# The low half of every second weight chunk formed by an accumulating DMA, in the gate blocks of a hybrid encoder

## Chip, cores and metric

One core of a Trainium2 chip runs the kernel as one program. The metric is device time in microseconds (us), the median of runs on the chip. Engines are named as in the profile: PE is TensorE (PEld its weight loads), DVE VectorE, ACT ScalarE, POOL GpSimd, SP SyncE, which issues most DMAs.

## The reference

One layer of an encoder on 256 tokens of width 2048, all in float32: an RMS norm, a wide input projection, two token mixers (a chunkwise mLSTM in both directions and an RG-LRU in both directions), each projected back to the model width, merged by sigmoid gates of the normalised input, and an output projection with a final norm.

```python
h = _rms_norm(x, norm_g)
proj = jnp.einsum('bsd,dn->bsn', h, w_in)
q_p, k_p, v_p, o_p, za_p, gif_p, xb_p, zb_p, ga_p, gb_p = jnp.split(proj, cuts, axis=-1)
ya = _mlstm_branch(q_p, k_p, v_p, o_p, za_p, gif_p, b_if, head_g)
yb = _rglru_branch(xb_p, zb_p, conv_w, conv_b, w_rg, b_rg, lam)
ya = jnp.einsum('bsw,wd->bsd', ya, w_branch_a)
yb = jnp.einsum('bsw,wd->bsd', yb, w_branch_b)
merged = jax.nn.sigmoid(ga_p) * ya + jax.nn.sigmoid(gb_p) * yb
out = _rms_norm(x + jnp.einsum('bsd,de->bse', merged, w_out), final_g)
```

The change touches the weights of the last lines but one: the columns of `w_in` for the gates `ga` and `gb`, `w_branch_a` and `w_branch_b`.

## The kernel before

The weights are read once, 512 columns at a time (a block of 2048 x 512, 4 MB), each block as eight chunks of 128 partitions x 1024 float32 (two slices of 128 rows side by side, 512 KB). PE multiplies in a rounded float32 type, so every operand is split in two: a high half `hi`, the value converted to that type, and a low half `lo`, what the conversion left out. A product takes three matmuls: high by high, high by low, low by high.

`load_chunk` makes a chunk's halves: SP loads it into `raw` (five buffers, L107), ACT converts it into `whi` (L108), DVE subtracts, `wlo = raw - whi` (L109). `whi` and `wlo` have three buffers each. `block_nat` (L112 to L126) uses the chunks as moving operand: 12 matmuls of 512 columns a chunk (L123 to L125, two slices by two token tiles by three products), 96 a block, into two PSUM accumulators. `block_tr` does the same with the chunks as stationary operand. The pairs of `load_chunk` carry a priority in the order of the program (`urgent`), and the Tile framework's scheduler, from priorities and its own estimates, fixes the order on each engine, PE's included, and sets the semaphores. Each engine then runs its own list in order.

The stage concerned is the last but one. For j = 0 to 3 it runs the block GB(j) of `wi`, then `wb[j]`; then for j = 0 to 3 the block GA(j) of `wi`, then `wa[j]`: 16 calls of `block_nat`, 128 chunks. Before it stand the four ZB blocks of `block_tr`, after it three `block_nat` blocks of `wo` and the last columns. After a block ACT or DVE takes the two accumulators over (sigmoid, L631 and L645; products, L637, L650, L651), and small transposes of the merged result are put between the chunks (L660). The slot `PT` (128 x 4096 float32) holds the attention weights until the last mLSTM head and later the scale `fg` of the final norm (loaded at L672, scaled by POOL at L673, first read at L688).

Of the kernel before, what the change touches and what calls it, by code (L numbers as in the profile page):

```python
# [10 lines left out]
F32 = mybir.dt.float32  # L11
F32R = mybir.dt.float32r
AF = mybir.ActivationFunctionType
ALU = mybir.AluOpType
ACT = mybir.EngineType.Activation

P = 128
# [3 lines left out]
NB = 512  # L21
KC = 2
# [6 lines left out]
BLK_Q, BLK_K, BLK_V, BLK_O, BLK_Z, BLK_XB, BLK_ZB, BLK_GA, BLK_GB = 0, 2, 4, 8, 12, 16, 20, 24, 28  # L29


def f(ap):
    return ap.bitcast(F32)
# [3 lines left out]
def hybrid_encoder(ctx: ExitStack, tc: tile.TileContext, x, xt, pk, bif, fg, wg, wi, wr, wa, wb, wo, out):  # L37
    nc = tc.nc
    pe, act, dve, pool, sp = nc.tensor, nc.scalar, nc.vector, nc.gpsimd, nc.sync
# [3 lines left out]
    wp = ctx.enter_context(tc.tile_pool(name="wp", bufs=1))  # L43
# [6 lines left out]
    def name(n):  # L50
        uid[0] += 1
        return f"{n}_{uid[0]}"
# [4 lines left out]
    def sl(tag, dt=F32, cols=4096):  # L57
        return slot.tile([P, cols], dt, tag=tag, name=name("s" + tag))

    def aux():  # L60
        return paux.tile([P, NB], F32, tag="aux", name=name("aux"))

    def acc_pair():
        return [pacc.tile([P, NB], F32, tag="acc", name=name("acc")) for _ in range(2)]

    def urgent():
        uid[0] += 1
        return tc.high_priority(offset=HP - 30 * uid[0])
# [10 lines left out]
    last_dma, last_copy, last_sub = [None], [None], [None]  # L79

    def tick():
        for q in (queue, queue2):
            if q:
                c = q.pop(0)
                if c is not None:
                    c()
# [9 lines left out]
    def load_chunk(src, dst=None, tag="w", bufs=3, parts=1):  # L96
        with urgent():
            raw = wp.tile([P, KC * NB], F32, tag="raw", name=name("raw"), bufs=5)
            if dst is None:
                hi = wp.tile([P, KC * NB], F32R, tag=tag + "hi", name=name(tag + "hi"), bufs=bufs)  # L100
                lo = wp.tile([P, KC * NB], F32R, tag=tag + "lo", name=name(tag + "lo"), bufs=bufs)
            else:
                hi, lo = dst
            w = KC * NB // parts
            for i in range(parts):
                r = slice(i * w, (i + 1) * w)
                last_dma[0] = sp.dma_start(raw[:, r], src[:, r]).ins  # L107
                last_copy[0] = act.copy(hi[:, r], raw[:, r]).ins  # L108
                last_sub[0] = dve.tensor_sub(lo[:, r], raw[:, r], f(hi[:, r])).ins  # L109
        return hi, lo  # L110

    def block_nat(src, xhi, xlo):  # L112
        ps = acc_pair()
        for kq in range(KT // KC):
            tick()
            hi, lo = load_chunk(src[kq])
            for kk in range(KC):
                k = kq * KC + kk
                wh, wl = hi[:, kk * NB:(kk + 1) * NB], lo[:, kk * NB:(kk + 1) * NB]
                for tb in range(2):  # L120
                    o = k * S + tb * P
                    a, b = xhi(o, o + P), xlo(o, o + P)
                    pe.matmul(ps[tb], a, wh, start=(k == 0), stop=False)  # L123
                    pe.matmul(ps[tb], a, wl, start=False, stop=False)  # L124
                    pe.matmul(ps[tb], b, wh, start=False, stop=(k == KT - 1))  # L125
        return ps  # L126

    def block_tr(src, xhi, xlo, pre=()):
        ps = acc_pair()
        for kq in range(KT // KC):  # L130
            tick()
            hi, lo = pre[kq] if kq < len(pre) else load_chunk(src[kq])
            for kk in range(KC):
                k = kq * KC + kk
                a, b = xhi(k * S, (k + 1) * S), xlo(k * S, (k + 1) * S)
                for m in range(4):
                    o = kk * NB + m * P
                    wh, wl = hi[:, o:o + P], lo[:, o:o + P]
                    dst = ps[m // 2][:, (m % 2) * S:(m % 2 + 1) * S]
                    first = k == 0 and m % 2 == 0  # L140
                    last = k == KT - 1
                    pe.matmul(dst, wh, a, start=first, stop=False, skip_group_check=True)  # L142
                    pe.matmul(dst, wh, b, start=False, stop=False, skip_group_check=True)  # L143
                    pe.matmul(dst, wl, a, start=False, stop=last, skip_group_check=True)  # L144
        return ps

    def evac_split(dst_hi, dst_lo, ps):
        with urgent():
            act.copy(dst_hi, ps)
            dve.tensor_sub(dst_lo, ps, f(dst_hi))  # L150
# [14 lines left out]
    hhi, hlo = Cols([hhi_t], 4096), Cols([hlo_t], 4096)  # L165
# [371 lines left out]
    def head(h):  # L537
        vhi = hp.tile([P, 2 * NB], F32R, tag="vhi", name=name("vhi"))
        vlo = hp.tile([P, 2 * NB], F32R, tag="vlo", name=name("vlo"))
        ps = block_nat(wi[BLK_V + h], hhi, hlo)  # L540
        for tb in range(2):
            r = slice(tb * NB, (tb + 1) * NB)
# [4 lines left out]
        to = hp.tile([P, 2 * NB], F32, tag="to", name=name("to"))  # L547
        zz = hp.tile([P, 2 * NB], F32, tag="zz", name=name("zz"))
        ps = block_nat(wi[BLK_O + h], hhi, hlo)
        with urgent():  # L550
            for tb in range(2):
                act.activation(to[:, tb * NB:(tb + 1) * NB], ps[tb], AF.Sigmoid, scale=rstd[:, tb:tb + 1])
        ps = block_nat(wi[BLK_Z + h], hhi, hlo)
        with urgent():
            for tb in range(2):
# [50 lines left out]
    ybh, ybl = [], []  # L606
    for j in range(4):
        ps = block_tr(wi[BLK_ZB + j], hhi, hlo)
# [14 lines left out]
    ybh, ybl = Cols(ybh, 1024), Cols(ybl, 1024)  # L623
    yah, yal = Cols([yas["h"]], 4096), Cols([yas["l"]], 4096)

    sgb = sl("E")
    for j in range(4):
        ps = block_nat(wi[BLK_GB + j], hhi, hlo)
        with urgent():
            for tb in range(2):  # L630
                act.activation(sgb[:, (j * 2 + tb) * NB:(j * 2 + tb + 1) * NB], ps[tb], AF.Sigmoid,  # L631
                               scale=rstd[:, tb:tb + 1])
        ps = block_nat(wb[j], ybh, ybl)
        with urgent():
            for tb in range(2):
                v = sgb[:, (j * 2 + tb) * NB:(j * 2 + tb + 1) * NB]
                dve.tensor_mul(v, v, ps[tb])  # L637

    mht, mlt = [], []
    for j in range(4):  # L640
        tg = hp.tile([P, 2 * NB], F32, tag="to" if j % 2 == 0 else "zz", name=name("tg"))
        ps = block_nat(wi[BLK_GA + j], hhi, hlo)
        with urgent():
            for tb in range(2):
                act.activation(tg[:, tb * NB:(tb + 1) * NB], ps[tb], AF.Sigmoid, scale=rstd[:, tb:tb + 1])  # L645
        ps = block_nat(wa[j], yah, yal)
        with urgent():
            for tb in range(2):
                v = tg[:, tb * NB:(tb + 1) * NB]
                dve.tensor_mul(v, v, ps[tb])  # L650
            dve.tensor_add(tg, tg, sgb[:, j * 1024:(j + 1) * 1024])  # L651
        mht.append(sl(f"C{j}", F32R, 1024))
        mlt.append(sl(f"D{j}", F32R, 1024))

        def fin_m(half, j=j, tg=tg):
            pt = aux()
            for i in range(2):
                m = half * 2 + i
                for tb in range(2):
                    pe.transpose(pt[:, i * S + tb * P:i * S + (tb + 1) * P],  # L660
                                 tg[:, tb * NB + m * P:tb * NB + (m + 1) * P], ident)
            o = half * NB
            evac_split(mht[j][:, o:o + NB], mlt[j][:, o:o + NB], pt)

        queue.extend([None, None, lambda c=fin_m: c(0), lambda c=fin_m: c(1)])
# [24 lines left out]
    for j in range(3):  # L690
        ps = block_nat(wo[j], mh, ml)
# [5 lines left out]
    for kq in range(8):  # L697
        o = (kq % 4) * KC * NB
        ch.append(load_chunk(wo[3][kq], dst=[lw[(kq // 4) * 2 + i][:, o:o + KC * NB] for i in range(2)]))
    for tb, a, b, col in ((0, 0, NB, 3), (1, 0, S, 3), (1, S, NB, 4)):  # L700
        ps = aux()[:, :b - a]
        for k in range(KT):
            hi, lo = ch[k // KC]
            c = (k % KC) * NB
            wh, wl = hi[:, c + a:c + b], lo[:, c + a:c + b]
            o = k * S + tb * P
# [58 lines left out]
```

## Time and profile before

| | us |
|---|---|
| runs (2) | 1052.97 and 1053.48, median 1053.22 |
| profiled execution, span from first to last instruction | 1050.9 |
| PE busy | 1039.4 (99%) |
| DVE busy | 646.9 (62%) |
| ACT busy | 533.5 (51%) |
| POOL busy | 36.7 (3%) |
| DMA, mean | 190 GB/s |

The span does not hold what the device does before the first and after the last instruction; the runs' times do, hence the 2.3 us between them. The busy time of PE counts a matmul from its start to its modelled end, and matmuls overlap. A group of instructions is shown as line, engine, operation, output and inputs, shape and count, then its busy time and the mean of one in nanoseconds, then the idle time of the engine just before such instructions and what ended it ("<-"). In the timeline a row gives the start, the duration, the instruction and, in brackets, the idle time before it and its releaser.

### The profile page before, as it was taken

To read this page: it belongs to the slowest core of one execution; us is meant where nothing else is said; L and a number is where in the kernel's file an instruction comes from. 1 tells how busy PE (TensorE), PEld (TensorE's weight loads), DVE (VectorE), ACT (ScalarE), POOL (GpSimd) and SP (SyncE) were. 2 spreads that over 40 slices of the span, in tenths; PEclk is the share of its full clock that TensorE was granted. 3 is DMA by queue.
4 is the path that set the end of the run, shared out by engine and by line. 5 is a ranking of instruction groups with operands and counts; after the bars stand their busy time and mean duration, and the time that the engine had idled before them with its cause. 6 is when DMAs were issued, how large, how long until landed. Compare 5 with 4: busy or idle time off the path is not lost.

```text
span 1050.9 us, 14840 instructions
## 1 busy us (share of the span) xinstructions
PE 1039.4 (99%) x5876; PEld 914.9 (87%) x5876; DVE 646.9 (62%) x809; ACT 533.5 (51%) x689; POOL 36.7 (3%) x48
## 2 busy tenths in 40 slices
PE   9999999999999999999999999999999999999996
PEld 8999988898889888988999988888888888888886
DVE  6566785489549845974786654454454545545573
ACT  7535447765684658466644443434434344444461
POOL 2000000010001001000320000000000000000000
PEclk9999999999999999999999999999999999999999
DMA  9744545556655654664656556666666565667652
GB/s 339 254 158 143 180 159 185 163 182 198 196 161 167 198 197 160 187 214 161 200 181 184 180 194 195 191 197 191 191 199 192 190 186 188 192 194 261 198 201 80
DMA packets 55669, 199.39 MB, mean 190 GB/s; under 512 B 6192, under 2 KB 6448, under 8 KB 55216
## 3 DMA queue, kind: packets, MB, share of 16 engines
q1 hardware_dynamic: 55600, 198.44, 58.7%
q8 instruction: 46, 0.75, 0.3%
q14 instruction: 23, 0.19, 0.0%
HBM read 196.32 MB, written 2.10 MB: 189 GB/s over the span
## 4 chain that ended last, share of the span: by engine, by line
PE 97%; DVE 1%; issue 1%; DMA 0%; POOL 0%; POOLq 0%; ACT 0%; DVEq 0%; SPq 0%; ACTq 0%
PE acc L123 21%; PE acc L124 21%; PE acc L125 21%; PE acc L144 9%; PE acc L142 9%; PE acc L143 9%; PE aux L573 1%; PE aux L490 1%; PE aux L489 1%; PE aux L488 1%; PE aux L403 1%; DVE sC L522 1%; PE aux L708 0%; PE aux L709 0%; PE aux L285 0%
## 5 line engine op out<-in xcount | busy, mean ns | idle before, releaser
L109 DVE TENSOR_TENSOR wlo<-raw,whi 128x1024 fp32r<-128x1024 f32 (+1 forms) x345 | 420.6, 1220 | 354.3 <-ACT whi L108 353.8
L108 ACT CAST whi<-raw 128x1024 fp32r<-128x1024 f32 (+1 forms) x345 | 361.7, 1049 | 442.2 <-PE acc L125 302.7
L124 PE MATMUL acc<-wlo,sH 128*128 128x512 f32 x640 | 249.7, 390 | 0.0
L125 PE MATMUL acc<-whi,sL 128*128 128x512 f32 x640 | 249.4, 390 | 0.0
L123 PE MATMUL acc<-whi,sH 128*128 128x512 f32 x640 | 229.5, 390 | 0.0
L142 PE MATMUL acc<-sH,whi 128*128 128x256 f32 x768 | 218.4, 286 | 0.8 <-ACT whi L108 0.8
L143 PE MATMUL acc<-sL,whi 128*128 128x256 f32 x768 | 217.0, 284 | 0.0
L144 PE MATMUL acc<-sH,wlo 128*128 128x256 f32 x768 | 215.0, 285 | 1.3 <-DVE wlo L109 1.3
L142 PEld LDWEIGHTS acc<-sH,whi 128*128 128x128 f32 x768 | 148.0, 193 | 2.0 <-ACT whi L108 1.1
L143 PEld LDWEIGHTS acc<-sL,whi 128*128 128x128 f32 x768 | 148.0, 193 | 0.3
L144 PEld LDWEIGHTS acc<-sH,wlo 128*128 128x128 f32 x768 | 146.1, 192 | 2.2 <-DVE wlo L109 2.0
L125 PEld LDWEIGHTS acc<-whi,sL 128*128 128x128 f32 x640 | 120.2, 188 | 24.4
L124 PEld LDWEIGHTS acc<-wlo,sH 128*128 128x128 f32 x640 | 120.3, 188 | 23.7
L123 PEld LDWEIGHTS acc<-whi,sH 128*128 128x128 f32 x640 | 119.9, 188 | 24.1
L124 PE MATMUL acc<-wlo,sC 128*128 128x512 f32 x224 | 87.2, 389 | 0.0
L125 PE MATMUL acc<-whi,sD 128*128 128x512 f32 x224 | 87.2, 389 | 0.0
L123 PE MATMUL acc<-whi,sC 128*128 128x512 f32 x224 | 78.4, 389 | 0.0
L124 PE MATMUL acc<-wlo,sA 128*128 128x512 f32 x128 | 49.8, 389 | 0.0
L125 PE MATMUL acc<-whi,sB 128*128 128x512 f32 x128 | 49.8, 389 | 0.0
L125 PEld LDWEIGHTS acc<-whi,sD 128*128 128x128 f32 x224 | 42.1, 188 | 8.7
L124 PEld LDWEIGHTS acc<-wlo,sC 128*128 128x128 f32 x224 | 42.1, 188 | 8.6
L123 PEld LDWEIGHTS acc<-whi,sC 128*128 128x128 f32 x224 | 42.0, 188 | 8.7
(221 smaller groups left out, 859.3 us busy)
## 6 DMA issues: line engine op xcount, KB each, us to landing
raw<-wi SPq DMA_DIRECT2D x255, 512.0 KB, 3.6
raw<-wb SPq DMA_DIRECT2D x32, 512.0 KB, 4.2
raw<-wa SPq DMA_DIRECT2D x32, 512.0 KB, 3.5
raw<-wo SPq DMA_DIRECT2D x32, 512.0 KB, 3.5
raw<-wr SPq DMA_DIRECT2D x8, 512.0 KB, 4.4
sA<-xt SPq DMA_DIRECT2D x8, 256.0 KB, 7.2
sB<-x SPq DMA_DIRECT2D x4, 512.0 KB, 8.4
sA<-x SPq DMA_DIRECT2D x1, 2048.0 KB, 9.1
```

The lines of the kernel that those rows point to most:

```text
L108: last_copy[0] = act.copy(hi[:, r], raw[:, r]).ins
L109: last_sub[0] = dve.tensor_sub(lo[:, r], raw[:, r], f(hi[:, r])).ins
L123: pe.matmul(ps[tb], a, wh, start=(k == 0), stop=False)
L124: pe.matmul(ps[tb], a, wl, start=False, stop=False)
L125: pe.matmul(ps[tb], b, wh, start=False, stop=(k == KT - 1))
L142: pe.matmul(dst, wh, a, start=first, stop=False, skip_group_check=True)
L143: pe.matmul(dst, wh, b, start=False, stop=False, skip_group_check=True)
L144: pe.matmul(dst, wl, a, start=False, stop=last, skip_group_check=True)
L403: pe.matmul(ps[:, tb * S:(tb + 1) * S], a, b, start=(n == 0), stop=(n == 5))
L488: pe.matmul(dst, whi[:, o:o + P], xh[:, r], start=True, stop=False)
L489: pe.matmul(dst, whi[:, o:o + P], xl[:, r], start=False, stop=False)
L490: pe.matmul(dst, wlo[:, o:o + P], xh[:, r], start=False, stop=True)
```

## The change

In the 16 blocks of this stage a chunk's number kq has a mode. Even chunks keep mode 0, the old way. Odd chunks have mode 1 in GB and in `wb[0]` and `wb[1]`, and mode 2 in `wb[2]`, `wb[3]`, GA and `wa`:

- mode 1: SP loads `raw` and ACT converts it into `hi` as before; ACT then writes `lo = -hi` and POOL issues a DMA that reads the chunk from HBM once more and adds it to `lo` (`accum_op=add`).
- mode 2: POOL issues the DMA that loads the chunk from HBM straight into `hi`, with conversion of type and without `raw`; the rest as in mode 1.

The pairs of buffers go round five: the three of `whi` and `wlo`, and two more cut out of the slot `PT`. So PT is taken again from the last head to the end of the stage.

```diff
+    wide = {"n": 0}
+
+    def load_wide(src, mode):
+        i = wide["n"] % 5
+        wide["n"] += 1
+        if i < 3:
+            hi = wp.tile([P, KC * NB], F32R, tag="whi", name=name("whi"), bufs=3)
+            lo = wp.tile([P, KC * NB], F32R, tag="wlo", name=name("wlo"), bufs=3)
+        else:
+            o = (i - 3) * 2048
+            hi, lo = wide["t"][:, o:o + 1024], wide["t"][:, o + 1024:o + 2048]
+        if mode == 0:
+            return load_chunk(src, dst=(hi, lo))
+        with urgent():
+            if mode == 1:
+                raw = wp.tile([P, KC * NB], F32, tag="raw", name=name("raw"), bufs=5)
+                last_dma[0] = sp.dma_start(raw, src).ins
+                act.copy(hi, raw)
+            else:
+                pool.dma_start(hi, src)
+            last_copy[0] = act.mul(lo, f(hi), -1.0).ins
+            pool.dma_start(lo, src, accum_op=ALU.add)
+        return hi, lo
+
-    def block_nat(src, xhi, xlo):
+    def block_nat(src, xhi, xlo, modes=None):
...
-            hi, lo = load_chunk(src[kq])
+            hi, lo = load_wide(src[kq], modes[kq]) if modes else load_chunk(src[kq])
...
+    wide["t"] = sl("PT", F32R)
+    ONE, TWO = (0, 1) * 4, (0, 2) * 4
     for j in range(4):
-        ps = block_nat(wi[BLK_GB + j], hhi, hlo)
+        ps = block_nat(wi[BLK_GB + j], hhi, hlo, ONE)
...
-        ps = block_nat(wb[j], ybh, ybl)
+        ps = block_nat(wb[j], ybh, ybl, ONE if j < 2 else TWO)
...
-        ps = block_nat(wi[BLK_GA + j], hhi, hlo)
+        ps = block_nat(wi[BLK_GA + j], hhi, hlo, TWO)
...
-        ps = block_nat(wa[j], yah, yal)
+        ps = block_nat(wa[j], yah, yal, TWO)
```

With 24 lines added ahead of it, `block_nat`'s three matmuls stand at L147 (high by high), L148 (with the low half of the weights) and L149 in the changed program.

On ACT's list, where the first mode-2 block (`wb[2]`) begins, the program before has only the conversions of the chunks, in order, with the two sigmoids of the block ahead between them; `raw` and `whi` are numbered by chunk:

```order
L108 CAST whi_1247_6826<-raw_1246_6825 128x1024
L108 CAST whi_1251_6844<-raw_1250_6843 128x1024
L631 ACTIVATE sE_1067_6082<-acc_1208_6675,rstd_142 128x512
L631 ACTIVATE sE_1067_6082<-acc_1209_6676,rstd_142 128x512
L108 CAST whi_1255_6862<-raw_1254_6861 128x1024
L108 CAST whi_1259_6880<-raw_1258_6879 128x1024
```

The changed program at the same place (sPT is the slot with the two further pairs; L132 is the negation, L657 the sigmoid):

```order
L108 CAST whi_1214_6814<-raw_1217_6816 128x1024
L108 CAST whi_1221_6849<-raw_1224_6851 128x1024
L132 ACTIVATE wlo_1219_6833<-whi_1218_6832 128x1024
L657 ACTIVATE sE_1067_6082<-acc_1185_6668,rstd_142 128x512
L657 ACTIVATE sE_1067_6082<-acc_1186_6669,rstd_142 128x512
L108 CAST sPT_1068_6083<-raw_1227_6882 128x1024
L132 ACTIVATE sPT_1068_6083<-sPT_1068_6083 128x1024
L108 CAST whi_1231_6915<-raw_1234_6917 128x1024
L132 ACTIVATE wlo_1229_6899<-whi_1228_6898 128x1024
```

Conversions of even chunks and negations of odd ones alternate, and the conversion of an even chunk (6849, kq = 2) stands ahead of the negation of the odd chunk before it (6833, kq = 1).

POOL's list had no DMA; from the last head to the scaling of `fg` it was empty:

```order
L580 TENSOR_TENSOR sq_906_5012<-sq_906_5012,rstd_142 128x1
L673 TENSOR_SCALAR sPT_1653_8510<-sPT_1653_8510 128x2048
L716 TENSOR_TENSOR ys_8517<-ys_8517,mhalf_140 128x1 x2
```

Now 104 DMAs stand between the first two of these; here those of `wb[2]` and the first of GB(3) (L131 loads a high half, L133 adds into a low half):

```order
L131 DMA whi_1218_6832<-wb 128x1024
L133 DMA wlo_1219_6833<-wb 128x1024
L131 DMA sPT_1068_6083<-wb 128x1024
L131 DMA whi_1228_6898<-wb 128x1024
L133 DMA sPT_1068_6083<-wb 128x1024
L131 DMA whi_1235_6933<-wb 128x1024
L133 DMA wlo_1229_6899<-wb 128x1024
L133 DMA wlo_1236_6934<-wb 128x1024
L133 DMA sPT_1068_6083<-wi 128x1024 x2
```

The first load is followed at once by its own add; behind it two loads at a time go ahead of their adds. The same pairs of a load with its own add directly behind it recur in `wb[3]` (7116, 7117), GA(0) (7354, 7355), GA(1) (7648, 7649) and GA(2) (7827, 7828).

PE's list in `wb[2]` before, at the chunk kq = 5 (acc_1243 and acc_1244 are the block's accumulators):

```order
L123 MATMUL acc_1243_6823<-whi_1267_6916,sC2_1026_5825 128x512
L123 MATMUL acc_1244_6824<-whi_1267_6916,sC2_1026_5825 128x512
L124 MATMUL acc_1243_6823<-wlo_1268_6917,sC2_1026_5825 128x512
L125 MATMUL acc_1243_6823<-whi_1267_6916,sD2_1027_5826 128x512
L124 MATMUL acc_1244_6824<-wlo_1268_6917,sC2_1026_5825 128x512
```

Now, with acc_1212 and acc_1213 for `wb[2]` and acc_1239 and acc_1240 for GB(3):

```order
L147 MATMUL acc_1212_6812<-whi_1228_6898,sC2_1026_5825 128x512
L147 MATMUL acc_1213_6813<-whi_1228_6898,sC2_1026_5825 128x512
L147 MATMUL acc_1239_6952<-sPT_1068_6083,sH_4_89 128x512
L147 MATMUL acc_1240_6953<-sPT_1068_6083,sH_4_89 128x512
L148 MATMUL acc_1239_6952<-sPT_1068_6083,sH_4_89 128x512
L149 MATMUL acc_1239_6952<-sPT_1068_6083,sL_5_90 128x512
```

The 12 matmuls of the next block's first chunk have moved in between the products with the high half of this odd chunk and those with its low half, which follow them.

## The prediction

> **What bounds the kernel now.** I read the page's first, second and fourth parts first, to see which engine carries the span.
>
> ```profile
> span 1050.9 us, 14840 instructions
> PE 1039.4 (99%) x5876; PEld 914.9 (87%) x5876; DVE 646.9 (62%) x809; ACT 533.5 (51%) x689; POOL 36.7 (3%) x48
> PEclk9999999999999999999999999999999999999999
> PE 97%; DVE 1%; issue 1%; DMA 0%; POOL 0%; POOLq 0%; ACT 0%; DVEq 0%; SPq 0%; ACTq 0%
> ```
>
> TensorE is busy in 99% of the span at the full granted clock, and the chain that ended last runs 97% through it. A busy PE need not be PE at its peak, so the next view is of the stage that the change touches: it lasts from about 602 us (last ZB block done) to about 954 us (the last product of a WA block is taken over). Columns are the stretch, its length, then busy time and count of PE, PEld, DVE, ACT, POOL, the granted clock, the DMA share and GB/s.
>
> ```profile
> 602.00:954.00 352.00, 352.00 (x1572) 291.94 (x1571) 177.76 (x158) 149.83 (x152) 0.00 (x0) 1.00 0.61 192
> ```
>
> PE never idles in those 352 us, DVE works half of them, ACT less, POOL not at all. What the engines wait for there:
>
> ```profile
> L108 ACT CAST whi<-raw 128x1024 fp32r<-128x1024 f32 x128 | 134.9, 1054 | 192.7 <-PE acc L125 188.4 <-PE acc L143 1.8 <-issue 1.6
> L109 DVE TENSOR_TENSOR wlo<-raw,whi 128x1024 fp32r<-128x1024 f32 x129 | 158.0, 1225 | 175.7 <-ACT whi L108 175.7
> 693.03 1.05 ACT L108 CAST whi<-raw 128x1024 fp32r<-128x1024 f32 x1 [1.66 <-PE acc L125]
> 695.75 1.05 ACT L108 CAST whi<-raw 128x1024 fp32r<-128x1024 f32 x1 [1.67 <-PE acc L125]
> 694.12 1.23 DVE L109 TENSOR_TENSOR wlo<-raw,whi 128x1024 fp32r<-128x1024 f32 x1 [1.50 <-ACT whi L108]
> ```
>
> The conversions wait for PE (ACT 188.4 us, for a buffer that a matmul still reads), DVE waits for ACT, and PE waits for neither. The rhythm is 695.75 - 693.03 = 2.72 us per chunk, the time of its 12 matmuls. DVE is done with the chunk at 695.35, and three pairs of buffers keep that ahead of PE. So the supply has slack and PE has none. Any change of supply gains nothing here, and costs as soon as its round trip exceeds its cover.
>
> **The change, part by part.**
>
> *Removed.* Of the 128 chunks in these 16 blocks the 64 odd ones lose their subtraction: 64 x 1.225 = 78 us of DVE. PE hides all of it today, so I cost it at 0. Outside the stage PE idles 1050.9 - 1039.4 = 11.5 us in all, in places that the change does not touch, and not even that would be 2%.
>
> *Added on ACT.* A negation of the shape of the conversion, 1.05 us. In 24 chunks (mode 1) it comes on top; in 40 (mode 2) it takes the conversion's place. ACT goes from 149.8 to about 175 us of 352: 0 as load. As a step in a chain it counts below.
>
> *Added on the DMA engines.* 64 chunks are read a second time, and 40 high halves go by POOL's queue instead of SP's. The trace has no DMA from POOL and none that adds, so I bound by what it has:
>
> ```profile
> raw<-wi SPq DMA_DIRECT2D x255, 512.0 KB, 3.6
> raw<-wb SPq DMA_DIRECT2D x32, 512.0 KB, 4.2
> raw<-wr SPq DMA_DIRECT2D x8, 512.0 KB, 4.4
> sB<-x SPq DMA_DIRECT2D x4, 512.0 KB, 8.4
> sPT<-fg SPq DMA_DIRECT2D x1, 1024.0 KB, 6.9
> 884.20:884.80 0.60, 0.60 (x4) 0.51 (x3) 0.60 (x1) 0.00 (x0) 0.00 (x0) 1.00 1.01 416
> ```
>
> The last number is microseconds from issue to landing. A casting load of 512 KB from POOL: between 3.6 (the same bytes in the quiet queue) and 8.4 (the same bytes behind others). I take 4.4, the row of a chunk that also enters an occupied queue. An adding transfer: between 3.6 (only the incoming bytes count) and 8.4. The destination must be read besides the source, 1024 KB in all, so I take the row with as many bytes, 6.9. POOL's own time for one issue is not seen; between 0 and 0.98, its time for a one-column operation (next fence).
>
> The Trainium skill, "Collectives: The Full Stack", section "The bandwidth ceiling: the fold count and why AG ≠ RS ≠ AR", says that an add in the DMA path costs nothing for the addition but needs two source reads, so that the rate halves. By it the sum is the one below; were an add as cheap as the raw row of wi, it would be about 0. No run here shows yet which holds.
>
> *Mode 1, steady (48 chunks).* Its chain begins when PE frees the pair of five chunks earlier: conversion 1.05, negation 1.05, adding transfer 6.9, three hand-overs of 0.1 (an estimate; the rows above show 0.04 from a conversion's end to the next start) = 9.3 us. Cover: the four chunks between, 4 x 2.72 = 10.88. Cost 0 at my price; at 8.4 it is 10.8 and still fits.
>
> *Entry.* The first odd chunk of GB0 cannot use that depth: its pair is one of the old three, freed by the next-to-last chunk of the last ZB block.
>
> ```profile
> 597.37 1.05 ACT L108 CAST whi<-raw 128x1024 fp32r<-128x1024 f32 x1 [1.83 <-PE acc L143]
> 600.25 1.05 ACT L108 CAST whi<-raw 128x1024 fp32r<-128x1024 f32 x1 [1.83 <-PE acc L143]
> L579 POOL TENSOR_TENSOR sq<-sq,mhalf 128x1 f32<-128x1 f32 x8 | 7.8, 980 | 0.7
> ```
>
> A ZB chunk lasts 600.25 - 597.37 = 2.88 us, so the cover is 2.88 + 2.72 = 5.6 against 9.3: **+3.7 us**, once (0 if the transfer takes 3.2 or less; +5.2 at 8.4).
>
> *Mode 2 (10 blocks, 80 chunks: wb from j = 2, all of GA and wa).* Here the high half itself is not fetched ahead: POOL may issue it only when the pair is free. Chain: load 4.4, negation 1.05, adding transfer 6.9, three hand-overs 0.3 = 12.65, against the same 10.88. An odd chunk n starts no earlier than the end of n - 5 plus 12.65; n - 5 is even and follows the odd n - 6. So six chunks take at least 2 x 2.72 + 12.65 = 18.09 us, 3.015 per chunk instead of 2.72: 80 x 0.295 = **+23.6 us**. A second loop closes nearly alike. ACT's order puts the conversion of chunk n + 1 ahead of the negation of n (the rows of its order in the section on the change), and that conversion waits for chunk n - 4: 2.72 + 1.05 + 1.05 + 6.9 + 0.2 = 11.92 in four chunks, 2.98 each. Queued behind the waiting negation are the conversions of the even chunks, and behind them DVE and PE. Both loops cost nothing if an adding transfer takes 5.1 (first loop, load at 4.4) or 5.86 us (second) or less; with 8.4 for both transfers the first gives 22.09 per six, 3.68 each, +77 us.
>
> *POOL's order.* It is a queue of its own in which a load waits for PE and an add for ACT. At five places of the mode-2 stage a load is followed at once by its own add, so the next load starts 4.4 + 1.05 + 0.2 = 5.65 us later plus POOL's issue, where two chunks give 5.44: 0.2 to 1.2 us each, partly inside the loop already. I take **+3**.
>
> *Moved.* The PT slot is held until the fourth-last chunk of wa, so the load of fg and POOL's scaling of it come out of the middle of the kernel.
>
> ```profile
> L673 POOL TENSOR_SCALAR sPT<-sPT x1: 10598/10598/10598, 521.6 to 521.6; 128x2048 f32<-128x2048 f32 x1
> L688 DVE TENSOR_TENSOR sA<-sA,sPT x7: 426/685/693, 979.0 to 1038.2; 128x512 f32<-128x512 f32 x6, 128x256 f32<-128x256 f32 x1
> ```
>
> Its first reader ran at 979.0, 25 us after the stage's end; the load (6.9) and the scaling (10.6) need 17.5, so 7 us are left even if the load waits for that end: 0. If that cover went, DVE would stand at L688 with the subtractions of the last blocks behind it.
>
> *Sum.* 3.7 + 23.6 + 3 = 30.3. The profiled execution's span is 1050.9, and the median of the runs, 1053.2, lies 2.3 above it (what surrounds a span); so 1053.2 + 30.3 = **1083.5 us**.
>
> **Rivals.**
>
> *The round trip is covered; no change.* Place: the same mode-2 loop; it decides at a load plus an add of 9.5 us together (10.88 less 1.35). With both at 3.6, the row of raw<-wi, they are 7.2: no stall, entry 5.6 against 6.0, hence 1053 to 1055; up to 1062 with adds at 5.5. For it: the rows of wi and wb land in 3.6 and 4.2. Against it: an add moves more than a raw does. The Trainium skill, "DMA: Bandwidth & Descriptors", section "Anatomy of one DMA — SWDGE (gpsimd) path", fits a POOL-issued transfer with about 2.0 us plus bytes over 436 GB/s, an estimate of 3.2 us for 512 KB; by that the sum would be about 0. It is a fit for copies, and nothing in this trace shows it.
>
> *The DMA engines become the bound.* Two chunks then carry a raw, a second load and an add with its read-back: four units of 512 KB in 5.44 us. While a transfer streams, the row 884.20:884.80 shows 416 GB/s at a share of 1.01, 1.26 us a unit: 5.04, just inside. But over the stage 192 GB/s are booked at a share of 0.61, which is 1.67 us a unit: 6.66 in 5.44, +1.22 for 64 pairs = +78, 1131. If an add counts three units, five by 1.67 are 8.33: +185, 1238. For it: 1.5 times the bytes at a share of 0.61 is 0.92 before any read-back. [...] It would slow the mode-1 blocks too, which the forecast leaves alone.
>
> *Faster.* PE's row would have to shrink: matmuls follow each other every 2.72/12 = 0.227 us at full clock whether DVE works or not. I see no mechanism worth 2%.
>
> **How the numbers follow.** Latency in the mode-2 loop, 1063 to 1110: 0.48. DMA engines as the bound, 1095 and up: 0.27. Covered, 1053 to 1062: 0.23. Faster: 0.02. 2% is 21 us, about what a measurement of this kernel tells from no change: 1074 is the edge. A seventh of the first case lies below it, so slower 0.41 + 0.27 = 0.68, same 0.30, faster 0.02. For the range I leave out the lower third of the covered case and the upper third of the saturated one: 1056 to 1165.
>
> **What would show it.** In the changed profile PE should idle in front of L148 (the product with the low half), released by DMAs into wlo and sPT, in mode-2 blocks and once near GB0, and hardly elsewhere. Blocks of mode 1 should keep 21.8 us, those of mode 2 rise to about 24. DVE should fall by 78 us. Adds should land in about 7 us, POOL's loads in 4.4. If PE waits in mode-1 blocks as well and the DMA share there nears 1, the saturated case is right; if adds land below 5 us and PE's idle time stays near 11 us, the covered one. I am wrong altogether if ACT or POOL proves the engine that paces the stage.

## Result and the profile after

The changed kernel takes **1142.75 us** (1142.68 to 1142.82, 2 runs) against 1053.22: the ratio is 1.085, 95% interval 1.082 to 1.088. The direction was forecast and the time lies in the range, but the loss is 89.5 us where 30.3 were forecast. The page of the changed kernel, the parts that answer to the first ones shown of before:

```profile
span 1141.1 us, 14917 instructions
PE 1070.8 (94%) x5876; PEld 932.1 (82%) x5876; DVE 568.9 (50%) x745; ACT 556.7 (49%) x713; POOL 110.9 (10%) x152
PE   9999999999999999999997999898887878899996
PEclk9999999999999999999998999998889987999999
PE 71%; issue 18%; DMA 5%; POOL 4%; ACT 1%; DVE 1%; POOLq 0%; SPq 0%; DVEq 0%; ACTq 0%
```

The span grew by 1141.1 - 1050.9 = 90.2 us. PE runs the same 5876 matmuls and is busy 1070.8 - 1039.4 = 31.4 us longer; its idle time went from 11.5 to 70.3 us, 58.8 more. The rows of 40 slices of 28.5 us show where: PE has gaps in the 22nd (599 to 628 us, the entry of the stage) and from the 26th on (713 us, where mode 2 begins), and in several of these slices its granted clock is no longer full. DVE fell by 646.9 - 568.9 = 78.0 us, as forecast, and that bought nothing. The first stretch below is the whole stage, the second the part of it from 720 us on, in which mode 2 is at work, with one block of mode 1 (GB(3)) among the others (columns as in the prediction):

```profile
602.00:1045.00 443.00, 383.73 (x1572) 308.51 (x1571) 101.94 (x93) 170.44 (x175) 82.59 (x104) 0.93 0.86 230
720.00:1045.00 325.00, 272.64 (x1089) 216.95 (x1088) 69.58 (x63) 104.83 (x110) 65.22 (x84) 0.92 0.82 214
```

The same 1572 matmuls that took 352 us now take 443, with PE busy 383.7 of them, at a mean clock of 0.93. Next, rows of the waits in the whole span (us in total, times, longest):

```profile
PE acc L148 <- DMA wlo<-wi: 24.2, 6, 6.9
POOL wlo L133 <- ACT wlo L132: 142.0, 30, 13.6
POOL whi L131 <- PE acc L149: 65.2, 18, 9.1
ACT wlo L132 <- DMA whi<-wi: 27.0, 6, 7.5
```

PE waits at L148, the product with the low half, for the adding transfer, as forecast; all rows of this kind together make 59.1 us. That transfer is issued late because POOL waits for ACT's negation, and the negation waits for POOL's load. The page's DMA issues (median us from issue to landing; into `wlo` go adds, into `whi` loads):

```profile
wlo<-wi POOLq DMA_DIRECT2D x19, 512.0 KB, 7.1
whi<-wi POOLq DMA_DIRECT2D x10, 512.0 KB, 6.6
whi<-wa POOLq DMA_DIRECT2D x10, 512.0 KB, 5.9
```

A load lands after 5.9 to 6.6 us in these rows and not 4.4. One such chain, from the timelines of PE, POOL and ACT; the first row is the last matmul that reads the pair which the load of 855.27 fills:

```profile
852.42 0.39 PE L149 MATMUL acc<-whi,sB 128*128 128x512 f32 x1
854.71 0.89 POOL L133 DMA_DIRECT2D sPT<-wa  x1 [5.56 <-ACT sPT L132]
855.27 0.89 POOL L131 DMA_DIRECT2D whi<-wi  x1
864.20 0.89 POOL L133 DMA_DIRECT2D wlo<-wi  x1 [4.96 <-ACT wlo L132]
864.77 0.89 POOL L131 DMA_DIRECT2D sPT<-wi  x1
862.84 1.06 ACT L132 ACTIVATE wlo<-whi 128x1024 fp32r<-128x1024 f32 x1 [5.77 <-DMA whi<-wi]
863.66 0.61 PE L147 MATMUL acc<-whi,sH 128*128 128x512 f32 x2
869.53 0.80 PE L148 MATMUL acc<-wlo,sH 128*128 128x512 f32 x1 [5.26 <-DMA wlo<-wi]
870.12 0.63 PE L149 MATMUL acc<-whi,sL 128*128 128x512 f32 x1
870.55 0.63 PE L148 MATMUL acc<-wlo,sH 128*128 128x512 f32 x1
```

The pair is free at 852.8 us, but its load goes at 855.27: it stands directly behind an add of another chunk, for which POOL had waited 5.56 us. The negation of 862.84 waits for this load, which lands after 7.5 us. The add of 864.20 waits for the negation, and the next load again stands directly behind that add: it goes at 864.77, with no wait of its own. The add lands when PE has been idle 5.26 us. From the free pair to the matmul of 869.53 it is 16.7 us, where four chunks give 10.9. In the whole trace 15 of POOL's 40 loads go directly behind an add for which POOL had waited, 70 us in all; these places are where the list itself costs time.

Behind the stall the matmuls follow each other in 0.43 us (870.55 - 870.12) instead of 0.227: the clock was halved. The prediction has no term for that. The Trainium skill, "TensorE: Matmul & The Clock Gate", section "Part 1: The HAM clock gate", gives half the clock after an idle window of about 3.4 us; the rows agree in that spacing nearly doubles after a stall of 5.3 us. The length of a stall alone does not settle it in these runs: in the changed kernel the spacing stays at 0.23 us behind a stall of 2.4 us (at 733.35 us), and run 10 below has slow matmuls behind one of 1.9 us.

### The profile page after: what moved, and what is told of

It reads as the page before. It is cut to its first block, busy times and chain, and to the rows that moved or that the text cites. A ratio compares the mean times of both kernels' runs of the same rounds, so it can differ in the third digit from the quotient of the medians.

```text
span 1141.1 us, 14917 instructions
## 1 busy us (share of the span) xinstructions
PE 1070.8 (94%) x5876; PEld 932.1 (82%) x5876; DVE 568.9 (50%) x745; ACT 556.7 (49%) x713; POOL 110.9 (10%) x152
## 4 chain that ended last, share of the span: by engine, by line
PE 71%; issue 18%; DMA 5%; POOL 4%; ACT 1%; DVE 1%; POOLq 0%; SPq 0%; DVEq 0%; ACTq 0%
PE acc L148 14%; PE acc L149 14%; PE acc L147 13%; PE acc L166 8%; PE acc L168 8%; PE acc L167 8%; DMA sPT<-wi 2%; DMA wlo<-wi 1%; POOL whi L131 1%; PE aux L597 1%; POOL sPT L133 1%; POOL wlo L133 1%; POOL sPT L131 1%; PE aux L514 1%; PE aux L513 1%
## 5 line engine op out<-in xcount | busy, mean ns | idle before, releaser
L109 DVE TENSOR_TENSOR wlo<-raw,whi 128x1024 fp32r<-128x1024 f32 (+1 forms) x256 | 314.0, 1228 | 373.1 <-ACT whi L108 372.6
L108 ACT CAST whi<-raw 128x1024 fp32r<-128x1024 f32 (+1 forms) x256 | 267.8, 1047 | 329.1 <-PE acc L149 161.7
L148 PE MATMUL acc<-wlo,sH 128*128 128x512 f32 x540 | 215.6, 399 | 24.3 <-DMA wlo<-wi 24.2
L149 PE MATMUL acc<-whi,sL 128*128 128x512 f32 x540 | 214.3, 397 | 0.0
L147 PE MATMUL acc<-whi,sH 128*128 128x512 f32 x540 | 200.7, 395 | 0.0
L148 PEld LDWEIGHTS acc<-wlo,sH 128*128 128x128 f32 x540 | 103.8, 192 | 47.7 <-DMA wlo<-wi 27.1
L149 PEld LDWEIGHTS acc<-whi,sL 128*128 128x128 f32 x540 | 103.9, 192 | 21.2
L147 PEld LDWEIGHTS acc<-whi,sH 128*128 128x128 f32 x540 | 102.9, 191 | 21.0
L109 DVE TENSOR_TENSOR sPT<-raw,sPT 128x1024 fp32r<-128x1024 f32 x25 | 30.6, 1225 | 120.9 <-ACT sPT L108 120.9
L148 PE MATMUL acc<-wlo,sC 128*128 128x512 f32 x176 | 68.7, 391 | 2.1 <-DMA wlo<-wb 2.1
L132 ACT ACTIVATE wlo<-whi 128x1024 fp32r<-128x1024 f32 x39 | 41.3, 1059 | 59.6 <-DMA whi<-wi 27.0
L149 PE MATMUL acc<-whi,sD 128*128 128x512 f32 x176 | 68.4, 389 | 0.0
L147 PE MATMUL acc<-whi,sC 128*128 128x512 f32 x176 | 64.8, 391 | 0.0
L108 ACT CAST sPT<-raw 128x1024 fp32r<-128x1024 f32 x25 | 26.2, 1048 | 52.7 <-PE acc L149 28.6
L148 PE MATMUL acc<-sPT,sH 128*128 128x512 f32 x100 | 41.1, 411 | 9.1 <-DMA sPT<-wi 9.0
```

Source lines behind the costliest of these rows:

```text
L132: last_copy[0] = act.mul(lo, f(hi), -1.0).ins
```

## The experiments

Beside them the kernel before took 1052.92 to 1053.14 us (medians); ratios are to it.

**1. The first form everywhere.**

```diff
-    ONE, TWO = (0, 1) * 4, (0, 2) * 4
+    ONE, TWO = (0, 1) * 4, (0, 1) * 4
```

> All 16 blocks in mode 1: SP loads raw, ACT converts and negates, POOL only issues the add. The bytes are those of the changed kernel (64 second reads, 64 adds); what goes is the load of the high half from POOL's queue. Round trip theory (load, negation and add one behind the other through POOL's queue exceed the four chunks of cover): only the entry stall of about 7 us and its 3.4 us of half clock stay, 1060 to 1068 us. Saturation theory (the DMA engines, at a share of 0.98, are the bound): the transfers are the same but for some 9% of the POOL loads, so most of the loss stays, 1110 to 1140 us.

Measured 1060.84 us, ratio 1.0074 (1.0059 to 1.0089). PE's longest wait:

```profile
PE acc L148 <- DMA wlo<-wi: 6.8, 1, 6.8
```

The same stretch as above (the stage ends at about 966 us here, so the last 80 us lie behind it):

```profile
720.00:1045.00 325.00, 325.00 (x1473) 269.54 (x1472) 122.02 (x119) 180.42 (x189) 43.01 (x44) 1.00 0.90 262
```

From the page, POOL's queue (packets, MB, share of the 16 DMA engines) and landings of two kinds of add:

```profile
q0 software_dynamic: 9216, 33.56, 17.1%
wlo<-wi POOLq DMA_DIRECT2D x19, 512.0 KB, 6.9
wlo<-wa POOLq DMA_DIRECT2D x10, 512.0 KB, 7.4
```

The bytes are those of the changed kernel, and PE has no gap in 325 us while the DMA engines move 262 GB/s, more than the change's 214. So the adds and the DMA engines are not what bounds mode 2. What is left is one stall of 6.8 us, the entry.

**2. The first block left as it was** (all its chunks in mode 0), the rest as changed.

```diff
-        ps = block_nat(wi[BLK_GB + j], hhi, hlo, ONE)
+        ps = block_nat(wi[BLK_GB + j], hhi, hlo, ONE if j else (0,) * 8)
```

> GB(0) keeps mode 0 in all eight chunks, so the ring of five pairs fills before the first add. Both theories: the entry stall (6.9 us idle and 6.8 us at half clock, 3.4 lost) goes and the rest stays, 1142.8 - 10.3 = 1132 us. If the half clock were no cost of its own, 1136.

Measured 1129.94 us (1126.72 to 1138.69), ratio 1.0742 (1.0696 to 1.0789): 12.8 us less than the changed kernel, with a spread about as wide. The stall of the entry is gone, the rest stays.

**3. Forty of SP's loads away.** In the blocks of mode 2 the even chunks are converted from a tile that stays in SBUF.

```diff
+        if mode == 3:
+            with urgent():
+                act.copy(hi, wide["keep"])
+                dve.tensor_sub(lo, wide["keep"], f(hi))
+            return hi, lo
...
-    ONE, TWO = (0, 1) * 4, (0, 2) * 4
+    ONE, TWO = (0, 1) * 4, (3, 2) * 4
```

> In the ten mode-2 blocks the even chunks convert one resident tile again and again instead of loading a chunk; this leaves 40 transfers out of the work, the mode-2 chain and POOL's queue stay. Contention theory (the chain is long because its load and add queue behind other transfers; alone they land in 4.2 and 5.3 us, the lowest seen, so 4.2 + 1.05 + 5.3 + 0.3 = 10.85 us against 10.88 of cover): the mode-2 stalls nearly go, 1065 to 1080 us. Order theory (POOL's list in order, with each load stuck behind an add that waits for ACT): more than 1110 us.

Measured 1117.67 us, ratio 1.0607 (1.0589 to 1.0625). A stretch with mode 2, and landings from the page:

```profile
720.00:1020.00 300.00, 261.31 (x1088) 208.03 (x1086) 71.36 (x66) 104.91 (x109) 65.34 (x82) 0.96 0.70 165
```

```profile
whi<-wi POOLq DMA_DIRECT2D x10, 512.0 KB, 6.2
wlo<-wa POOLq DMA_DIRECT2D x10, 512.0 KB, 5.5
```

25 of the 90 us go, as the order theory had it (more than 1110). At a share of 0.70, with these loads of SP gone, PE still idles 39 us in 300. Contention stretches the chain; it doesn't make it.

**4. Mode 2 without its add** (40 of the 64 left out).

```diff
-            pool.dma_start(lo, src, accum_op=ALU.add)
+            if mode == 1:
+                pool.dma_start(lo, src, accum_op=ALU.add)
```

> As the changed kernel, but in mode 2 the add is left out (the low half is only the negated high half). The chain is load 4.2 to 6.6, negation 1.05, hand-overs 0.2: at most 7.9 us against 10.88. Round trip theory: the mode-2 loss goes, 1062 to 1068 us with the entry. If loads from POOL by themselves, or the negation's place in ACT's order, held the stage up, more than 1080 us.

Measured 1061.24 us, ratio 1.0075 (1.0058 to 1.0092), the same as run 1. Loads and POOL's queue on the page:

```profile
whi<-wi POOLq DMA_DIRECT2D x10, 512.0 KB, 4.8
whi<-wa POOLq DMA_DIRECT2D x10, 512.0 KB, 4.5
q0 software_dynamic: 9216, 33.56, 12.1%
```

A load from POOL without adds behind it lands in 4.5 to 4.8 us (close to the 4.4 of the forecast), and alone costs nothing; nor does an add alone (run 1). Only the load and the add in one chain, on one list, cost some 80 us. Two theories stood then. *Round trip*: a pair, once free, needs 6.6 + 1.05 + 6.6 + 0.3 = 14.55 us to be full again, more than its cover. *Lists*: each of POOL and ACT works through its own list in order, and instructions that could go on stand behind others that wait for a transfer.

**5. Six pairs of buffers** (the sixth from two tiles that are idle by then).

```diff
-        i = wide["n"] % 5
+        i = wide["n"] % 6
...
+        elif i == 5:
+            hi = hp.tile([P, KC * NB], F32R, tag="vhi", name=name("vhi"))
+            lo = hp.tile([P, KC * NB], F32R, tag="vlo", name=name("vlo"))
```

> The changed kernel with a sixth buffer pair in the four groups (the two 4 KB tiles that held v's halves, idle by then). Round trip theory: in the changed kernel load and add both land after a median of 6.6 us, so that a pair that TensorE frees is full again 14.55 us later (6.6 + 1.05 + 6.6 + 0.3), against a cover of four chunks, 10.88 us. With six pairs the cover is 13.6 us, six chunks take at least 2.72 + 14.55 = 17.27 us, 2.88 each instead of 2.72: about 13 us of idle TensorE in the 80 chunks of the second form, 6 to 10 us of half clock behind it, and the entry's 8 us: 1075 to 1090 us. List theory (what counts is that a load stands behind an add in GpSimd's list, however many pairs there are): at most a tenth of the loss comes back, 1130 us or more. Bandwidth theory (the accumulating transfers fill the DMA engines): the same bytes, 1130 us or more.

**6. Seven pairs in the last two groups**, six in the first two.

```diff
+        elif i == 6:
+            hi, lo = sl("C3", F32R, 1024), sl("D3", F32R, 1024)
...
+    wide["n"], wide["p"] = 0, 7
     for j in range(4):
         tg = ...
```

> Six pairs in the first two groups as in the run before, and seven in the last two, the seventh being the tiles C3 and D3, which are empty between the second group and the end of the last. Round trip theory: with seven pairs eight chunks take at least 5.44 + 14.55 = 20.0 us, 2.50 each, under TensorE's 2.72: no stall in the 64 chunks of the last two groups, 2 to 3 us in the 16 chunks of the second form that have six pairs, and the entry's 8 us: 1061 to 1070 us. List theory and bandwidth theory: 1120 us or more, as with six.

Measured 1124.67 us, ratio 1.0689 (1.0663 to 1.0715), with six, and 1120.08, ratio 1.0647 (1.0626 to 1.0669), with seven. The round trip alone doesn't explain this: seven pairs cover 16.3 us, and 67 us of loss stay. With the slower landings of run 6's own page (loads from `wi` into `whi` 9.0 us, adds 6.9) the round trip is 17.3 us, which by the same sum costs some 8 us in 64 chunks. Nor does the list theory's bound quite hold: 1120 for seven is just on it, and six are 5 us below the 1130. In the two traces 23 and 20 of the 40 loads go directly behind an add that had waited, against 15 in the changed kernel.

**7. Every fourth chunk in the second form**, the other odd ones in the first.

```diff
-    ONE, TWO = (0, 1) * 4, (0, 2) * 4
+    ONE, TWO = (0, 1) * 4, (0, 2, 0, 1) * 2
```

> The changed kernel with only every fourth chunk in the second form where it had every second, the other in the first form (copy by ScalarE, load by SyncE): 20 loads by GpSimd instead of 40, the same 64 adds, bytes and pairs. Round trip theory: a chain of two chunks of the second form now spans eight chunks, 5.44 + 5.44 + 14.55 = 25.43 us against 21.76 of TensorE: 3.18 each, +37 us of idle, 10 to 20 us of half clock and the entry's 8: 1105 to 1120 us. A theory by which every load through GpSimd costs its own share (82 us over 40 loads): half of it and the entry, 1100 us. A theory by which only loads that stand close behind one another's adds are late: 1065 to 1085 us.

Measured 1137.56 us, ratio 1.0806 (1.0790 to 1.0822): half the loads, and nearly the whole loss. All three expectations were too low. One turn, from the timelines of POOL, ACT and PE (L129 is the first form's conversion):

```profile
792.97 0.56 POOL L131 DMA_DIRECT2D whi<-wi  x1 [2.40 <-PE acc L149]
801.72 0.86 POOL L133 DMA_DIRECT2D wlo<-wi  x1 [8.19 <-ACT wlo L132]
800.37 1.06 ACT L132 ACTIVATE wlo<-whi 128x1024 fp32r<-128x1024 f32 x1 [1.60 <-DMA whi<-wi]
801.33 1.04 ACT L129 CAST whi<-raw 128x1024 fp32r<-128x1024 f32 x1
808.67 0.63 PE L148 MATMUL acc<-wlo,sH 128*128 128x512 f32 x1 [2.84 <-DMA wlo<-wi]
```

Here POOL's list holds nothing up: the load goes when PE frees its pair, and the matmul follows 15.7 us later, against four chunks of 10.9. The negation at 800.37 waits for the load, and behind it on ACT's list stands the conversion of a chunk of the first form (801.33), so that list hands the lateness on to a chunk that doesn't use the load. But PE doesn't stall for it: followed back from add to load, all 16 stalls of more than 0.3 us behind 720 us stand before low halves of the second form. What was mis-sized is the round trip. The page has loads into `whi` landing after 8.3 to 8.6 us here and adds into `wlo` after 7.2 to 8.2; with 8.4 and 7.4 it is 17.15 us, eight chunks take at least 10.88 + 17.15 = 28.0, and the 80 chunks lose 63 us. With the entry's 9.0 (run 8) that is an estimate of 1125, before any half clock. Why loads land later here than in the changed kernel stays open.

**8. The first form everywhere, and the first block left as it was** (the edits of runs 1 and 2).

```diff
+    ONE, TWO = (0, 1) * 4, (0, 1) * 4
...
+        ps = block_nat(wi[BLK_GB + j], hhi, hlo, ONE if j else (0,) * 8)
```

> Every second chunk in the first form throughout, as in the run where all are of that form, and the first block of the first group left as it was (all chunks split by VectorE). If the 7.6 us of that run above the kernel before are the entry's stall with its half clock, and nothing else in the first form costs, this gives 1052 to 1055 us, with TensorE never idle for over 0.5 us in the four groups. If the stall only moves to the second block, where the adds begin with no lead either, 1058 to 1062 us.

Measured 1051.80 us, ratio 0.9991 (0.9982 to 1.0001): no difference from before, with PE without a gap through the stage:

```profile
602.00:955.00 353.00, 353.00 (x1571) 292.27 (x1570) 105.00 (x98) 211.39 (x211) 56.09 (x61) 1.00 1.00 283
```

The entry is therefore worth 1060.84 - 1051.80 = 9.0 us, and 60 accumulating transfers otherwise cost nothing where they are not chained to loads, even at a DMA share of 1.00.

**9. Seven pairs, and the lists laid down.** Every chunk's load or conversion is now written two chunks ahead, and for chunk n of mode 2:

```diff
+                if n + 1 in wide["cp"]:
+                    st.enter_context(tc.issue_after(wide["cp"][n + 1]))
+                if n + 2 in wide["ld"]:
+                    st.enter_context(tc.issue_after(wide["ld"][n + 2]))
+                negate_add(n)
```

`cp` and `ld` hold the conversion and the load of a chunk; `issue_after` puts ACT's negation and POOL's add behind these on their lists.

> The pairs of the run with seven (six in the first two groups, seven in the last two), with the two lists laid down: GpSimd's add for a chunk of the second form stands behind the load for the chunk two later, and ScalarE's negation behind the copy for the chunk one later, so that nothing that could go on stands behind an instruction that waits for a transfer. Without this, loads stood behind adds that waited for ScalarE, and ScalarE's copies behind negations that waited for loads. List theory: the add is due 10.9 us after its place in the list comes free and needs some 8.5, and the round trip of 14.55 us lies within seven pairs' 16.3 us: no stall in the last two groups, 1 to 4 us in the 16 chunks with six pairs, and the entry's 8 us unless the earlier issue takes some of it: 1053 to 1068 us. Theory that the lists are nothing and the transfers too slow (contention in the DMA engines): as with seven pairs before, 1110 to 1125 us.

Measured 1082.14 us, ratio 1.0278 (1.0262 to 1.0293): 38 us less than run 6 with the same pairs. What POOL waited for from 720 to 1045 us, first in run 6 (L136 loads, L138 adds, L137 negates), then in run 9 (L146, L130, L129):

```profile
POOL wlo L138 <- ACT wlo L137: 84.7, 15, 10.8
POOL sPT L138 <- ACT sPT L137: 45.6, 10, 11.2
POOL vlo L138 <- ACT vlo L137: 39.0, 7, 10.4
POOL sPT L136 <- PE acc L154: 12.2, 5, 5.0
```

```profile
POOL whi L146 <- PE acc L176: 45.8, 15, 9.2
POOL sPT L146 <- PE acc L176: 35.9, 12, 5.0
POOL wlo L130 <- ACT wlo L129: 25.6, 12, 4.7
POOL sPT L130 <- ACT sPT L129: 24.7, 12, 5.1
POOL vlo L130 <- ACT vlo L129: 16.1, 7, 5.3
```

In run 6 POOL stood at adds that waited for ACT (169 us in these rows), and its loads waited little for PE (12.2 us in the row shown, 28.5 in all); now the loads wait for a free pair (81.7 us in two rows), as they should, none goes directly behind an add that waited, and the adds wait 66. PE keeps two large stalls, 7.5 us at the entry and 8.1 at the start of the third group, so the 1053 to 1068 expected was missed by 14 us.

**10. The same lists with five pairs.**

```diff
-        i = n % 6 if n < 64 else (n - 64) % 7
+        i = n % 5
```

> The same two lists with the change's five pairs. List theory: here the load for the chunk two later waits for TensorE to free its pair, and the add behind it then lands some 8.5 us later (0.6 for the load's issue, 1.05 for the negation, 0.3, and 6.6), where TensorE has only two chunks, 5.4 us, to do: 3.1 us of idle for each of the 40 chunks of the second form, some 120 us with half clock on top of it: 1170 to 1220 us. Theory that only the round trip and the number of pairs count, and the lists don't: 1142 us, as the changed kernel. Theory of the DMA engines: 1142 us or a little less.

Measured 1148.79 us (1142.44 to 1151.81), ratio 1.0900 (1.0861 to 1.0939). No better than the change, and far from the 1170 expected; the number alone is nearest to the theory that only the round trip and the pairs count. From the timelines, a stall, the last matmul before a pair comes free, the load that this releases, the add behind it, that chunk's negation, and the matmul that waits for the add:

```profile
856.78 0.50 PE L175 MATMUL acc<-wlo,sA 128*128 128x512 f32 x1 [1.94 <-DMA wlo<-wa]
863.29 0.39 PE L176 MATMUL acc<-sPT,sB 128*128 128x512 f32 x1
863.98 0.56 POOL L146 DMA_DIRECT2D sPT<-wi  x1 [7.40 <-PE acc L176]
864.52 0.91 POOL L130 DMA_DIRECT2D wlo<-wi  x1
861.46 1.06 ACT L129 ACTIVATE wlo<-whi 128x1024 fp32r<-128x1024 f32 x1
872.79 0.80 PE L175 MATMUL acc<-wlo,sH 128*128 128x512 f32 x1 [3.67 <-DMA wlo<-wi]
```

The mechanism is the expected one (the add waits behind a load that waits for PE), but its price was wrong in two places. The negation was done 2 us before, at 862.5, so its 1.05 us isn't in the sequence. And PE stalls at every second odd chunk, not at each: the loop runs from one stall to the next and holds four chunks. PE's work until the pair is free takes 7.2 us, the load's issue 0.54, and the add lands 8.2 us after that: 16.0 us where four chunks take 10.88. Half clock is part of the loop: from 856.78 to 863.29 PE starts 22 matmuls, whose 21 spacings would take 4.8 us at 0.227 and take 6.5, so 1.7 of the 5.1 us lost in this turn are the clock's. The five turns from 795 to 873 us last 15.2 to 16.0 us each; at that rate the 80 chunks of mode 2 would lose 87 to 103 us (an estimate), and less the entry's 9.0 the loss is 1148.8 - 1053.1 - 9.0 = 86.7.

**11. Run 9 with the first block left as it was.**

```diff
-        ps = block_nat(wi[BLK_GB + j], hhi, hlo, ONE)
+        ps = block_nat(wi[BLK_GB + j], hhi, hlo, ONE if j else (0,) * 8)
```

> The ordered lists with seven pairs, and the first block left as it was before the change (all chunks split by VectorE), which took the entry's stall away in the first form. List theory: all three causes gone, 1050 to 1058 us, no difference from the kernel before, with 40 loads and 60 adds by GpSimd and TensorE hardly idle. Otherwise 8 us under the run with ordered lists.

Measured 1074.73 us (1069.79 to 1076.82), ratio 1.0189 (1.0164 to 1.0215): 7.4 less, not the 1050 to 1058. One row of PE's timeline says what is left:

```profile
799.98 0.79 PE L175 MATMUL acc<-wlo,sH 128*128 128x512 f32 x1 [10.02 <-DMA wlo<-wi]
```

**12. The numbering of pairs carried on** where the seventh comes in; until then a chunk there got the pair used four chunks before.

```diff
-        i = n % 6 if n < 64 else (n - 64) % 7
+        i = n % 6 if n < 64 else (4, 5, 0, 1, 2, 3, 6)[(n - 64) % 7]
```

> The run before (ordered lists, seven pairs, first block left as it was), which kept one stall of 10.0 us at the start of the third group. There the numbering of the pairs starts anew with the seventh, so that a chunk gets the pair that the chunk four before it used, not the one seven before. Here the numbering goes on with the pair that has been idle longest; nothing else differs. If that stall is the renumbering's alone, its 10 us and the half clock behind it (some 2 us) go: 1058 to 1064 us, the rest being the small stalls in the 16 chunks that have six pairs. If it is the group's own (two blocks' ScalarE work, the switch to other inputs), it stays: 1072 to 1077 us.

Measured 1065.38 us (1063.65 to 1068.10), ratio 1.0121 (1.0102 to 1.0141), 1.4 us above the range expected; the stall of 10 us is gone. A stretch with mode 2, and lines of the page:

```profile
720.00:960.00 240.00, 232.92 (x1023) 188.34 (x1022) 66.28 (x62) 98.76 (x104) 56.59 (x78) 1.00 1.01 270
```

```profile
PE 1043.7 (98%) x5876; PEld 913.5 (86%) x5876; DVE 572.4 (54%) x749; ACT 551.2 (52%) x709; POOL 106.5 (10%) x148
wlo<-wi POOLq DMA_DIRECT2D x11, 512.0 KB, 8.0
```

The transfers land even later than in the changed kernel (adds into `wlo` after 8.0 us against 7.1), the DMA engines are booked full, and PE idles 7 us in 240 at full clock. So neither the transfers' speed nor the DMA engines' load by itself cost the 80 us: it took five pairs and the lists. Of the 12.0 us of span left, 7.7 are PE's gaps, none over 2 us in the stage, and 4.3 are PE's busy time (1043.7 against 1039.4); why that is longer at full clock stays open.

## Why the prediction was right or wrong

- *What bounds the kernel; DVE's 78 us at nothing*: right. DVE fell by 78.0 us, and in run 8 DVE's work of the stage is 40% lower with no difference in time.
- *Mode 1, steady, at 0*: right. Adds land in 6.9 to 7.5 us in run 1 (6.9 was taken), and run 8 is level with before. In the changed kernel one chunk of GB(3), between blocks of mode 2, stalls PE 2.4 us; its add took 9.0.
- *Entry, +3.7*: the place right, the size not. PE stalled 6.9 us in the changed kernel and 6.8 in run 1. The add that it waits for lands 9.3 us after its issue in the changed kernel (603.41 to 612.71), where 6.9 were taken; with the clock halved behind the stall the entry is worth 9.0 us (run 8).
- *The mode-2 loop, +23.6*: this is a step that failed, by the size of a term. The load was taken at 4.4 us, from a row of SP's queue. It lands in 5.9 to 6.6 us when it shares POOL's queue with adds, and in 4.5 to 4.8 without (run 4). With 6.6 for load and add the loop closes in 5.44 + 14.55 = 20.0 us for six chunks, 3.33 each, +49 us instead of +24. But that formula isn't the law of the stage: by it six pairs should have given some 1075 to 1090 and gave 1124.67. (The loop at 8.4 us for both transfers has a slip: 5.44 + 8.4 + 1.05 + 8.4 + 0.3 = 23.59 us for six chunks, +97 us; the 22.09 and +77 hold for a load of 8.4 and an add of 6.9.)
- *POOL's order, +3*: **the step that failed most**. It was counted as five places, with 0.2 to 1.2 us each, where a load has its own add directly behind it. But any load that stands behind an add of mode 2 waits for that add's negation, and so for an earlier load: 15 of the 40 loads go directly behind an add that had waited, 70 us in all. POOL is busy only 65 of 325 us there; it is the order of its list that counts, not its load. With five pairs neither order is good. The load of chunk n + 2 may go when PE frees a pair, two chunks (5.44 us) before chunk n begins, while the add of n must go some 6.6 us before chunk n begins. Put the add first, and the load waits for the earlier load, its negation and the add's issue: 6.6 + 1.05 + 0.56 and two hand-overs of 0.3 in all, 8.5 us for two chunks instead of 5.44 (an estimate; no run has this order throughout). Put the load first, and four chunks take some 15.5 us instead of 10.88 (run 10). The change's list mixes both and loses (1142.8 - 1053.2 - 9.0) / 40 = 2.0 us per two chunks. Seven pairs undo the conflict, and then the order decides: 1120 us without it, 1082 with it, 1065 when the entry and the renumbering are mended too. Run 9 laid down ACT's list and POOL's together and wrote the loads two chunks ahead; what each is worth apart wasn't tried.
- *The conversions queued behind a waiting negation*: named, but not priced. Run 7 shows such a conversion in its rows, but no stall of PE that comes from it; what this path costs in the changed kernel wasn't shown.
- *No term for the clock*: PE is busy 31.4 of the 90.2 us longer, and its rows behind the long stalls show half clock. Where a single stall stands by itself it is an addition (the entry, 9.0 for 6.8). In run 10 it lies inside the loop as well, 1.7 of 5.1 us in the turn shown, because a pair comes free later when the matmuls before that are slow. How much would be saved in the changed kernel if the clock stayed full wasn't shown.
- *The DMA engines as the bound (1131)*: the number came near the result, the mechanism didn't hold. Run 1 moves the same bytes with no stall but the entry's, and run 12 has a DMA share of 1.01 in mode 2 with 7 us of idle PE. The Trainium skill's rule in "Collectives: The Full Stack", section "The bandwidth ceiling: the fold count and why AG ≠ RS ≠ AR", that an add in the DMA path needs two source reads, agrees with the rows. 64 adds are 17.1% x 16 x 1058.7 = 2897 us of DMA engine time in run 1, 45 us each. Run 4 has 40 loads and 24 such adds in 12.1% x 16 x 1059.8 = 2052 us, which leaves 24 us a load if an add books as much there. An add books 1.9 times the time of a load.
- *Covered (1053 to 1062)*: true of mode 1 (run 8), and nearly of seven pairs in order (run 12, 1065), not of the change: load and add take 6.6 us each there, 13.2 together, where it needed 9.5.

## What to carry to other kernels

A round trip against its cover is only half the sum when both transfers of it are issued from one in-order list: write down who stands behind the instruction that waits, on every list that the chain crosses, and ask whether any order lets the loads go ahead; if a load's buffer comes free later than the add before it must go, more buffers are needed first, and then the order has to be laid down. Price a transfer in the queue and company that it will have, not by its quietest row. Count how many chunks lie between one stall and the next before you price a loop, and put the slow clock behind the stall into it. When the engine that bounds a kernel is already full, taking work from another engine brings nothing: the best form of this change is level with the kernel before.

## What the runs showed that was not expected

- A POOL-issued transfer shows POOL busy for 0.56 us if it is a load (up to 0.91 directly behind an add) and 0.86 to 1.09 if it is an add; but the next one on the list starts 0.54 to 0.57 us after it in the rows above (863.98 and 864.52, 864.20 and 864.77).
- Behind a stall of 5 to 7 us PE ran at half clock, spacing 0.43 us instead of 0.227, and in run 10 behind one of 1.9 us too; run 12, whose gaps in the stage are 2 us at most, kept a full clock throughout.
- At a DMA share of 1.00 over 353 us PE had no gap (run 8): a full share of the DMA engines did not by itself mean that anything waited for them.
